# A recurrent mixer's 64x64 inverses: block transposes moved from the matmul array to VectorE, and output products regrouped

## The chip, the cores and the metric

One core of a Trainium2 chip runs the whole program; the other cores are idle. The metric is the device time of one execution in microseconds (us). The engines that matter here are TensorE (PE: the matmuls, with the loading of their stationary operands shown apart as PEld), VectorE (DVE) and ScalarE (ACT). Each works through its own list of instructions in a fixed order, and they wait for one another by semaphores. Matmul results land in PSUM, a memory of eight banks; DVE and ACT carry them from there to on-chip memory (SBUF).

## The reference

The input x has 512 tokens of 1024 features. Three blocks follow one another: a macaron block (half a SwiGLU feed-forward, a mixer, half a feed-forward), a second block with a gated recurrence and spatial gating, and a third with two more layers. All is in float32. The change lies in the first block's mixer alone, and there in its recurrent half:

```python
p = h @ w_in                                  # r, k, v and the inputs of small low-rank products
w = -softplus(-(w0 + tanh(w_lo) @ w2)) - 0.5
a = sigmoid(a0 + a_lo @ a2)
kk = normalised (k * k_k) per head;  bh = kk * a;  decay = exp(-exp(w))
def step(state, inp):                          # 8 heads, state 64 x 64, 512 tokens
    sa = einsum('bhvk,bhk->bhv', state, -kk_t)
    state = state * w_t[:, :, None, :] + sa[..., None] * b_t[:, :, None, :] + v_t[..., None] * k_t[:, :, None, :]
    return state, einsum('bhvk,bhk->bhv', state, r_t)
o = normalised per head, plus a bonus, times a gate
```

The other half of the mixer is sliding-window attention; both halves go through w_out onto the residual.

## The kernel before, in words

**The dense products.** Every large product (`dense_steps`, lines 348 to 365) splits float32 into two float32r parts and issues three matmuls with 512 moving columns for each K tile: L359, L360 and L361. They are called a triple below. The weights come by DMA into `raw`, are split by ACT (L335) and DVE (L336), and stand in `whi` and `wlo`.

**The recurrence.** Tokens are cut into 8 chunks of 64, heads into 4 pairs. Inside a chunk the recurrence needs the inverse of a unit triangular 64x64 matrix, one for each head and chunk. `head` (lines 867 to 974) computes one head's eight inverses at once: tile X (128 partitions x 4 x 64) holds the eight transposed inverses, chunk j,e on partition half e. It starts from diagonal blocks of 4 (two rounds of matmuls at L928, two updates at L929) and doubles the block size four times: blocks of 8, 16, 32, 64. A doubling, called a level below, takes W = mask * (ak' X) (matmuls L942, DVE L945), then X -= T' W on the odd blocks (matmuls L949, DVE L951; at the last level DVE L957 and ACT L958 write the result to `xb`). T is X transposed, so it has to be made anew ahead of every level. That is `turned()`, called four times for each of the eight heads, 32 times in all: for each of the eight 64x64 blocks a product with an identity, L921 in transpose mode for the blocks on partitions 0 to 63 and L919 as an ordinary float32 matmul for those on 64 to 127, alternating; then ACT copies all from PSUM to T (L922). As the doubling goes, X is block-diagonal with blocks of at most 32 whenever it is turned.

**States and outputs.** `states` (from line 977) makes, for a pair of heads, three groups of small products over the chunks (L991), a chain of six steps from chunk to chunk (matmul L1008, DVE L1009), and the outputs `po`: for each of 2 heads and 8 chunks two products into the same 64x64 patch, one from `gv` and `rb` with 128 rows and 64 columns (L1018), then one from the state `z` and `cf` with 64 rows and 64 columns (L1019), one chunk after the other. `finish` (from line 1025) normalises and gates what they give.

A float32 matmul of the program runs as two MATMUL instructions on PE, a product in transpose mode as one; so L919 counts 256 instructions in the trace, L921 128, L942 and L949 512 each, L1018 and L1019 128 each. The profile's "64*64" or "128*64" is the part of the array that an instruction uses (rows*columns).

**What sets the order.** Five generators are stepped in turn by `rounds` in the pattern D Z A D H P H A: D the dense projections (one triple a step; at the end the product with w_out), Z the states, A the attention, P what is done per token, H the heads. The order of emission is thus fixed in the program, with dense triples between the heads' small products as long as D has work. D stands still where the product with w_out has to wait for the states of the third pair. A scheduler then orders each engine's list near that emission. Each engine keeps its list's order whatever is ready.

Of the kernel before, what the change touches and what calls it, by code (L numbers as in the profile page):

```python
# [12 lines left out]
AF = mybir.ActivationFunctionType  # L13
# [13 lines left out]
# ---------------------------------------------------------------- layout and shape-only constants  # L27

def col_blocks(w, cols=None):
    """(K, N) -> (N/128, 128, K/128 * 128): one 128-column block holds its K tiles side by side."""  # L30
    k, n = w.shape
    return np.ascontiguousarray(
        w.reshape(k // P, P, n // P, P).transpose(2, 1, 0, 3).reshape(n // P, P, (k // P) * P))


def wide_blocks(w):
    """(1024, N) -> (N/512, 4, 128, 2 * 512): 512 columns of two K tiles to a block"""
    n = w.shape[1]
    return np.ascontiguousarray(
        w.reshape(4, 2, P, n // S, S).transpose(3, 0, 2, 1, 4).reshape(n // S, 4, P, 2 * S))  # L40


def masks_1():
    t = np.arange(P)
    # rows are tokens of a chunk, on either half of the partitions
    s, u = (t % 64)[:, None], np.arange(64)[None, :]
    out = {"up": s < u, "upi": s <= u, "m4u": (s // 4 == u // 4) & (s < u), "m4l": (s // 4 == u // 4) & (s > u), "id2": s == u}
    for l in range(2, 6):
        # columns of the odd blocks only
# [16 lines left out]
class Pack:  # L66
    """Column-packed (128, n) array with named column ranges."""
# [25 lines left out]
def down(w):  # L93
    """(F, 1024) -> list over groups of F tiles of (8, 128, n * 128)"""
# [33 lines left out]
def layout_3(i, a, vec, at):  # L128
# [26 lines left out]
    c = Pack()  # L155
# [5 lines left out]
    # retention: even and odd dimensions of a head in tiles of their own  # L161
# [6 lines left out]
    # the last head's rows by themselves, whole  # L168
# [21 lines left out]
def layout(inputs):  # L190
# [27 lines left out]
    # the last two recurrent heads by themselves  # L218
# [13 lines left out]
# ---------------------------------------------------------------- the program  # L232

class Model:
# [21 lines left out]
    def setup(self):  # L256
# [27 lines left out]
        # the first blocks of weights come between the tiles of x  # L284
# [8 lines left out]
    def banks(self, **n):  # L293
        """the PSUM banks of a phase: how many to a tag"""
# [10 lines left out]
    def spill(self):  # L305
        """the residual waits in DRAM; its place on chip serves the mixer meanwhile"""
# [8 lines left out]
    def sooner(self, n):  # L315
        """n instructions ahead of its place in the scheduler's order"""
# [4 lines left out]
    # -- dense products ------------------------------------------------  # L321
# [5 lines left out]
    def weights(self, src):  # L327
        """a (128, n <= 1024) block of weights as an exact sum of two float32r parts"""
# [10 lines left out]
    def dense(self, blocks, act, tag="d"):  # L339
        """blocks: list of (weights src, first K tile of act, n K tiles); returns the accumulated tile"""  # L340
# [7 lines left out]
    def dense_steps(self, blocks, act, tag="d", every=NKT):  # L348
        """the same, with a pause after every so many K tiles"""
# [26 lines left out]
    # -- norms ---------------------------------------------------------  # L376
    def ln_exp(self):
        """the one table set that serves both Ln and Exp"""
# [5 lines left out]
    def in_turn(self, i):  # L384
        """ACT issues the instructions given here in their order, to change tables seldom"""
# [5 lines left out]
    def newton(self, y, m, tmp):  # L391
        """one step for y = m ** -0.5"""
# [6 lines left out]
    def rsqrt_(self, out, m, tmp):  # L399
        """out = m ** -0.5 for positive m"""  # L400
        nc = self.nc
        with self.ln_exp():
            # Ln serves 2 ** -64 to 2 ** 64
# [4 lines left out]
    def rsqrt_few(self, out, m, tmp):  # L408
        """the same for a few numbers per partition"""
# [3 lines left out]
    def norm_in(self, g):  # L413
        """split of x * g and the running sum of squares, K tile by K tile"""
# [15 lines left out]
    def sum_sq(self, acc, x, k):  # L430
        """acc += x * x, from k = 0 on; returns the square"""
# [9 lines left out]
    def token_sums(self, acc, out, scale, bias):  # L441
        """out (128 tokens, 4 blocks) = scale * sum over the partitions of acc (128, 512), or of several, + bias"""
# [9 lines left out]
    def spread(self, pool, rt, tag):  # L452
        """(128 tokens, 4 blocks) -> (128, 512) with that row on every partition"""
# [17 lines left out]
    def rstd(self, acc, eps, meanwhile=lambda: None):  # L471
        """1 / sqrt(mean over the 1024 features + eps), on every partition; meanwhile(): products
        that keep the tensor engine busy until it can be spread"""
# [8 lines left out]
    def norm_twice(self, pool, g1, g2, eps1, eps2):  # L482
        """the split of the residual times both gains, and a function for when the first product is under
        way (meanwhile: as in rstd): it returns the factor per token that completes both norms, and a function that puts the norm
        by g1 in the residual's place"""
# [47 lines left out]
    def token_dense_steps(self, w, act, evac, step=None):  # L533
        """products with tokens on partitions: w is (N / 512, 4, 128, 2 * 512), two K tiles to a block;
        evac(column block, token block, tile). Token block n is tokens 128 n.., or n, n + 4, .. by step"""
# [18 lines left out]
    def conv(self, out, b, w, bias, j, n):  # L554
        """causal depthwise convolution of width 4 over the tokens; b has three zeros in front"""
# [6 lines left out]
    def residual(self, w, act, c0=0):  # L562
        """x += act @ w, over the K tiles of w from column c0 of its blocks"""
# [5 lines left out]
    # -- feed-forward --------------------------------------------------  # L569
# [49 lines left out]
# ---------------------------------------------------------------- RWKV-7 and sliding-window attention  # L619
# [9 lines left out]
def weave(*gens, tc=None, ahead=None):  # L629
    """emits the generators' steps in turn until all have ended; ahead: by how many  # L630
    instructions each goes before its place in the scheduler's order"""
# [12 lines left out]
def rounds(gens, order):  # L644
    """steps of the named generators in the given order, again and again until all have ended"""
# [6 lines left out]
class Mixer1:  # L652
# [22 lines left out]
    # banks for the heads, for what is per token, and for states and outputs  # L675
# [9 lines left out]
    def shifted(self, j, out, swap=False):  # L685
        """projection tile j, scaled by the norm, mixed with the token before;
# [290 lines left out]
    def states(self, i, q):  # L977
# [35 lines left out]
        for h in range(2):  # L1013
# [6 lines left out]
            if h == 0:  # L1020
                yield
# [1204 lines left out]
```

## Time and profile before

| what | value |
|---|---|
| median of the three runs | 2947.56 us (2942.62 to 2950.02) |
| span of the profiled execution, first to last instruction | 2940.8 us |
| the profiled execution's own time | not listed apart; the runs lie 1.8 to 9.2 us above the span |
| PE busy | 2897.1 us, 99% of the span |
| DVE busy | 1675.2 us, 57% |
| ACT busy | 1174.8 us, 40% |
| mean clock granted to PE | 0.979 |
| stretch of the mixer's recurrence | about 410 to 845 us from the start |

The share of busy time of PE counts a matmul from its start to its modelled end, and neighbours overlap. What an instruction costs PE's list is therefore read here from the timeline, as the distance from its start to the start of the next row; this is called its pitch. The granted clock (PEclk) is 1.00 at full speed.

### The profile page before, as it was taken

Reading aid. Unit: us, or ns where it says so; the run is one execution under the profiler, and the core shown is the slowest. Engines: PE = TensorE matmul, PEld = TensorE weight load, DVE = VectorE, ACT = ScalarE, POOL = GpSimd, SP = SyncE. Lnnn points to the kernel's source line nnn. Section 1 sums busy time; section 2 is a strip of 40 time slices with the busy share of each in tenths; the row PEclk is TensorE's granted clock in tenths of the full one; section 3 lists DMA queues with packets and bytes.
Section 4 is the critical chain, followed back from the end, with each engine's and each line's share of the span. In section 5 each row is a group of like instructions: output and inputs, shape, how many; then the busy total and the mean of one; then the engine's idle time right before and its main releaser. Section 6 shows DMA issues by size and latency. Waiting matters only on the chain. (4 is left out here: it accounts for less than half of the span.)

```text
span 2940.8 us, 37140 instructions
## 1 busy us (share of the span) xinstructions
PE 2897.1 (99%) x14918; PEld 2331.2 (79%) x14918; DVE 1675.2 (57%) x2762; ACT 1174.8 (40%) x1813; POOL 78.9 (3%) x167
## 2 busy tenths in 40 slices
PE   8999999999999999999999999999999999999998
PEld 7888867777768888877888878888887777888887
DVE  5444565556254344768535697545834895555456
ACT  4222353444232222456423334434527544343333
POOL 0000000000000000000000011110000000000000
PEclk9999999999699999999999999999989999999999
DMA  4333331001023333432233344444212543322232
GB/s 139 94 101 93 93 110 37 23 27 43 20 65 95 99 95 95 143 95 79 85 102 129 108 128 153 137 135 124 92 45 79 172 143 122 115 79 79 69 108 76
DMA packets 83870, 281.24 MB, mean 96 GB/s; under 512 B 10097, under 2 KB 10609, under 8 KB 82929
## 3 DMA queue, kind: packets, MB, share of 16 engines
q1 hardware_dynamic: 76464, 255.28, 28.1%
q0 software_dynamic: 5888, 18.09, 1.8%
q10 hardware_dynamic: 1344, 5.49, 0.5%
q8 instruction: 117, 1.92, 0.3%
q14 instruction: 57, 0.46, 0.0%
HBM read 254.44 MB, written 23.07 MB: 94 GB/s over the span
## 5 line engine op out<-in xcount | busy, mean ns | idle before, releaser
L335 ACT CAST whi<-raw 128x1024 fp32r<-128x1024 f32 (+4 forms) x454 | 450.5, 992 | 1194.9 <-PE ps_d L360 795.2
L359 PE MATMUL ps_d<-xhi,whi 128*128 128x512 f32 x1896 | 759.2, 401 | 12.9 <-ACT whi L335 8.4
L361 PE MATMUL ps_d<-xhi,wlo 128*128 128x512 f32 x1896 | 746.0, 394 | 3.4 <-DVE wlo L336 3.4
L360 PE MATMUL ps_d<-xlo,whi 128*128 128x512 f32 x1896 | 746.3, 394 | 0.0
L336 DVE TENSOR_TENSOR wlo<-raw,whi 128x1024 fp32r<-128x1024 f32 (+4 forms) x454 | 521.9, 1149 | 167.5 <-ACT whi L335 166.6
L359 PEld LDWEIGHTS ps_d<-xhi,whi 128*128 128x128 f32 x1896 | 358.3, 189 | 93.8 <-ACT whi L335 8.8
L361 PEld LDWEIGHTS ps_d<-xhi,wlo 128*128 128x128 f32 x1896 | 358.6, 189 | 80.4 <-DVE wlo L336 4.8
L360 PEld LDWEIGHTS ps_d<-xlo,whi 128*128 128x128 f32 x1896 | 358.9, 189 | 74.5 <-issue 3.7
L359 PE MATMUL ps_d<-hh,whi 128*128 128x512 f32 x608 | 237.5, 391 | 0.6 <-ACT hh L373 0.6
L361 PE MATMUL ps_d<-hh,wlo 128*128 128x512 f32 x608 | 237.2, 390 | 0.5 <-DVE wlo L336 0.5
L360 PE MATMUL ps_d<-hl,whi 128*128 128x512 f32 x608 | 237.2, 390 | 0.3 <-DVE hl L374 0.3
L361 PEld LDWEIGHTS ps_d<-hh,wlo 128*128 128x128 f32 x608 | 114.2, 188 | 25.0 <-DVE wlo L336 1.4
L359 PEld LDWEIGHTS ps_d<-hh,whi 128*128 128x128 f32 x608 | 114.2, 188 | 24.9 <-ACT hh L373 1.0
L360 PEld LDWEIGHTS ps_d<-hl,whi 128*128 128x128 f32 x608 | 114.2, 188 | 24.6 <-DVE hl L374 1.1
L594 DVE TENSOR_TENSOR hb<-ps_d,rstd 128x512 f32<-128x512 f32 x44 | 30.4, 691 | 136.2 <-PE ps_d L361 136.2
L601 DVE SCALAR_TENSOR_TENSOR x<-ps_d,x 128x512 f32<-128x512 f32 x48 | 33.2, 692 | 116.3 <-PE ps_d L361 116.3
L359 PE MATMUL ps_d<-mixhi,whi 128*128 128x512 f32 x224 | 89.0, 397 | 1.0 <-DVE x L1641 0.8
L360 PE MATMUL ps_d<-mixlo,whi 128*128 128x512 f32 x224 | 88.3, 394 | 0.0
L361 PE MATMUL ps_d<-mixhi,wlo 128*128 128x512 f32 x224 | 88.1, 393 | 0.0
L593 DVE TENSOR_TENSOR ha<-ps_d,rstd 128x512 f32<-128x512 f32 x44 | 30.4, 692 | 95.8 <-PE ps_d L361 93.2
L438 DVE TENSOR_TENSOR acc<-acc,sq 128x512 f32<-128x512 f32 x67 | 46.1, 688 | 25.7 <-ACT sq L437 25.1
L1445 DVE TENSOR_TENSOR x<-ps_d,x 128x512 f32<-128x512 f32 x32 | 22.0, 689 | 61.3 <-PE ps_d L361 61.3
(698 smaller groups left out, 4441.3 us busy)
## 6 DMA issues: line engine op xcount, KB each, us to landing
raw<-in_ffn_gu_dram SPq DMA_DIRECT2D x88, 512.0 KB, 3.6
raw<-in_w_in_dram SPq DMA_DIRECT2D x64, 512.0 KB, 3.6
raw<-in_ffn_dn_dram SPq DMA_DIRECT2D x32, 512.0 KB, 3.6
raw<-in_w_up_dram SPq DMA_DIRECT2D x32, 512.0 KB, 3.7
raw<-in_w_down_dram SPq DMA_DIRECT2D x32, 512.0 KB, 4.0
raw<-in_ret_in_dram SPq DMA_DIRECT2D x32, 512.0 KB, 3.3
raw<-in_ab_in_dram SPq DMA_DIRECT2D x28, 512.0 KB, 3.4
raw<-in_ret_v_dram SPq DMA_DIRECT2D x16, 512.0 KB, 3.3
```

Source lines behind the costliest of these rows:

```text
L335: nc.scalar.copy(hi[:, :n], raw[:, :n])
L336: nc.vector.tensor_sub(lo[:, :n], raw[:, :n], hi[:, :n].bitcast(F32))
L359: self.nc.tensor.matmul(ps, lhsT=hi[:, w], rhs=ah, start=first, stop=False)
L360: self.nc.tensor.matmul(ps, lhsT=hi[:, w], rhs=al, start=False, stop=False)
L361: self.nc.tensor.matmul(ps, lhsT=lo[:, w], rhs=ah, start=False, stop=last)
L438: nc.vector.tensor_add(acc, acc, sq)
L593: nc.vector.tensor_mul(a, pg, r)
L594: nc.vector.tensor_mul(b, pu, r)
L601: nc.vector.scalar_tensor_tensor(out=xm, in0=po, scalar=0.5, in1=xm, op0=ALU.mult, op1=ALU.add)
L1445: nc.vector.tensor_add(xm, po, xm)
```

## The change

Two edits in the recurrent half of the mixer. `turned()` no longer goes through PE, PSUM and ACT: one DVE instruction transposes the 32x32 blocks of X into T, each block in its place, for all eight matrices. Because X is block-diagonal with blocks of at most 32 there, this is the transpose that the level needs. In `states` the 16 products of `gv` and `rb` come first, then a step of the generator ends, then the 16 products of `z` and `cf`. So that the patches of one PSUM bank can stand open meanwhile, only the first product of each head carries the flag that starts an accumulation and only the last the flag that ends it. The number of steps of each generator is the same as before. The change also drops comments and docstrings, most of them without moving a line; from `turned()` on, lines stand 7 lower than before (L942 is now L935, L949 now L942, L1018 now L1011), and from `finish` on 3 lower.

```diff
         def turned():
-            pt = half(self.pm())
-            for j, e, he in each:
[...]
-                if e:
-                    mm(pt[he, j], lhsT=X[he, j], rhs=m.const("ident")[he, he], start=True, stop=True)
-                else:
-                    nc.tensor.transpose(pt[he, j], X[he, j], m.const("ident")[he, he])
-            nc.scalar.copy(T, pt)
+            nc.vector.transpose(T.rearrange("p j t -> p (j t)"), X.rearrange("p j t -> p (j t)"))
...
         po = self.pz()
         for h in range(2):
             hs = HALF[h]
             rb = q["rb%d" % h]
             for c in range(8):
+                mm(po[hs, c * 64:c * 64 + 64], lhsT=gv[:, c, hs], rhs=rb[:, c], start=(c == 0), stop=False,
+                   skip_group_check=True)
+        yield
+        for h in range(2):
+            hs = HALF[h]
+            for c in range(8):
                 cs = slice(c * 64, c * 64 + 64)
-                mm(po[hs, cs], lhsT=gv[:, c, hs], rhs=rb[:, c], start=True, stop=False)
-                mm(po[hs, cs], lhsT=z[hs, c], rhs=cf[hs, cs], start=False, stop=True)
-            if h == 0:
-                yield
+                mm(po[hs, cs], lhsT=z[hs, c], rhs=cf[hs, cs], start=False, stop=(c == 7), skip_group_check=True)
         self.step[i] = 2
         yield from self.finish(i, q, po)
```

On PE, in the first level of the first two heads, the list before ran as follows (`x8` stands for eight equal rows; X, T, W and ak are the tiles named above, `xhi` and `whi` belong to a dense triple, `cst` holds the identity):

```order
L942 MATMUL ps_m<-X,ak 64x32 x8
L949 MATMUL ps_m<-W,T 64x32 x8
L359 MATMUL ps_d<-xhi,whi 128x512
L360 MATMUL ps_d<-xlo,whi 128x512
L361 MATMUL ps_d<-xhi,wlo 128x512
...
L949 MATMUL ps_m<-W,T 64x32 x8
L921 MATMUL ps_m<-cst,X 64x64
L919 MATMUL ps_m<-cst,X 64x64
...
L359 MATMUL ps_d<-xhi,whi 128x512
```

The same place now:

```order
L935 MATMUL ps_m<-X,ak 64x32 x8
L942 MATMUL ps_m<-W,T 64x32 x8
L359 MATMUL ps_d<-xhi,whi 128x512
L360 MATMUL ps_d<-xlo,whi 128x512
L361 MATMUL ps_d<-xhi,wlo 128x512
...
L942 MATMUL ps_m<-W,T 64x32 x8
L359 MATMUL ps_d<-xhi,whi 128x512
```

The pairs of L921 and L919 (four pairs to a group) are gone and nothing has come in their place on PE; the triples stand where they stood. In the recurrence's whole stretch of PE's list the dense matmuls are 584 before and 584 now.

On DVE, at the same place, the list before (L929 are the updates of X in blocks of 4, L951 those of a level, L1056 belongs to the attention):

```order
L929 SCALAR_TENSOR_TENSOR X<-ps_m,m_2450 128x256 x2
L1056 TENSOR_TENSOR z<-ps_d,rstd 128x512
L929 SCALAR_TENSOR_TENSOR X<-ps_m,m_2450 128x256
L336 TENSOR_TENSOR wlo<-raw,whi 128x1024
L945 TENSOR_TENSOR W<-ps_m,m_2450 128x128 x2
L951 TENSOR_TENSOR X<-X,ps_m 128x32x4 x2
```

DVE's list at that place now, where L922 is the old L929, L938 the old L945 and L944 the old L951:

```order
L922 SCALAR_TENSOR_TENSOR X<-ps_m,m_2450 128x256 x2
L915 STREAM_TRANSPOSE T<-X 128x256
L1053 TENSOR_TENSOR z<-ps_d,rstd 128x512
L922 SCALAR_TENSOR_TENSOR X<-ps_m,m_2450 128x256
L336 TENSOR_TENSOR wlo<-raw,whi 128x1024
L915 STREAM_TRANSPOSE T<-X 128x256
L938 TENSOR_TENSOR W<-ps_m,m_2450 128x128 x2
L944 TENSOR_TENSOR X<-X,ps_m 128x32x4
L915 STREAM_TRANSPOSE T<-X 128x256
```

Each transpose stands right behind the update of X that it reads, or one instruction later, and ahead of the W of the same level.

On PE, the first pair's outputs before (`gv`, `rb`, `z` and `cf` as above):

```order
L361 MATMUL ps_d<-xhi,wlo 128x512
L1018 MATMUL ps_z<-rb,gv 64x64
L1019 MATMUL ps_z<-cf,z 64x64
...
L359 MATMUL ps_d<-xhi,whi 128x512
```

PE's list for the same outputs now, where L1011 is the old L1018 and L1018 the old L1019:

```order
L1011 MATMUL ps_z<-rb,gv 64x64 x16
L359 MATMUL ps_d<-xhi,whi 128x512
L360 MATMUL ps_d<-xlo,whi 128x512
L361 MATMUL ps_d<-xhi,wlo 128x512
...
L1018 MATMUL ps_z<-cf,z 64x64 x16
```

Before, a run of eight alternating pairs stood here, and the second head's run came some rows later; now 16 products of one kind stand together, and the 16 of the other kind come where the second run was.

## The prediction

> **What bounds the kernel now.** I read the page's totals, the windows over the mixer, PE's waits there, and the groups and timeline of the instructions that go.
>
> ```profile
> span 2940.8 us, 37140 instructions
> PE 2897.1 (99%) x14918; PEld 2331.2 (79%) x14918; DVE 1675.2 (57%) x2762; ACT 1174.8 (40%) x1813; POOL 78.9 (3%) x167
> ```
>
> ```profile
> 425.00:450.00 25.00, 25.00 (x317) 18.59 (x316) 9.70 (x21) 8.03 (x15) 0.15 (x1) 1.00 0.10 24
> 700.00:725.00 25.00, 24.25 (x327) 19.34 (x325) 21.78 (x68) 11.18 (x32) 0.00 (x0) 1.00 0.17 70
> 725.00:750.00 25.00, 25.00 (x193) 17.80 (x192) 6.38 (x19) 4.58 (x12) 0.00 (x0) 0.65 0.13 38
> 750.00:775.00 25.00, 25.00 (x202) 16.71 (x201) 7.56 (x16) 7.52 (x15) 0.15 (x1) 0.67 0.00 1
> 775.00:800.00 25.00, 25.00 (x194) 19.08 (x191) 6.77 (x13) 6.23 (x16) 0.00 (x0) 0.73 0.13 38
> 400.00:850.00 450.00, 444.59 (x3769) 318.41 (x3767) 234.30 (x571) 170.63 (x352) 1.69 (x15) 0.90 0.11 35
> ```
>
> Columns: stretch, its length, busy time of PE, PEld, DVE, ACT and POOL, granted clock, DMA share, GB/s. PE is occupied for 444.6 of the mixer's 450 us while DVE has 234 and ACT 171. All the same the DVE is nearly full in one place, 21.8 of 25 us from 700 on.
>
> ```profile
> PE ps_m L928 <- DVE X L929: 0.5, 1, 0.5
> ```
>
> ```profile
> DVE W L945 <- PE ps_m L942: 53.8, 26, 4.8
> ACT T L922 <- PE ps_m L919: 77.5, 31, 6.6
> ```
>
> Columns: who waited for whom, total us, times, longest. On the inverse and the outputs PE waited for another engine once, 0.5 us; DVE and ACT waited for PE. So inside the mixer time is PE's list added up, at the clock that it is granted. What leaves that list leaves the time, unless PE then has to wait.
>
> **The transposes, PE.** The groups that go, and one of them in the timeline at full clock and one at the lower:
>
> ```profile
> L919 PE MATMUL ps_m<-cst,X 64*64 64x64 f32 x256 | 43.3, 252 | 0.0
> L921 PE MATMUL ps_m<-cst,X 64*64 64x64 f32 x128 | 31.9, 250 | 0.0
> L922 ACT COPY T<-ps_m 128x256 f32<-128x256 f32 x32 | 11.9, 372 | 77.5 <-PE ps_m L919 77.5
> ```
>
> ```profile
> 431.12 0.24 PE L921 MATMUL ps_m<-cst,X 64*64 64x64 f32 x1
> 431.29 0.33 PE L919 MATMUL ps_m<-cst,X 64*64 64x64 f32 x2
> ...
> 432.58 0.33 PE L919 MATMUL ps_m<-cst,X 64*64 64x64 f32 x2
> 432.83 0.50 PE L359 MATMUL ps_d<-xhi,whi 128*128 128x512 f32 x1
> ...
> 747.84 0.31 PE L921 MATMUL ps_m<-cst,X 64*64 64x64 f32 x1
> ...
> 750.00 0.47 PE L919 MATMUL ps_m<-cst,X 64*64 64x64 f32 x2
> 750.40 1.22 PE L1035 MATMUL ps_m<-wsg,lora 128*128 128x512 f32 x1
> ```
>
> The busy time, 75.2 us, counts overlaps twice. By pitch a group lasts 432.83 - 431.12 = 1.71 us at full clock and 750.40 - 747.84 = 2.56 at the lower. Added over all 384 instructions, from 431.12 to 779.61, the pitches give 53.6 us, 1.68 to each of 32 groups. The triples around them stay, and the number of switches between dense and small runs is about the same in both lists (123 and 121 dense runs), so nothing is gained there: **-53.6 us**.
>
> **The transposes, DVE.** 32 instructions of 128x256 come; ACT's 11.9 us go. No row shows a DVE transpose. Its nearest rows are operations of that size from SBUF to SBUF, the far one the scan of twice the size:
>
> ```profile
> L1113 DVE TENSOR_SCALAR sc<-sc,asm 128x256 f32<-128x256 f32 x24 | 7.4, 350 | 0.2
> L901 DVE TENSOR_TENSOR X<-X,m 128x256 f32<-128x256 f32 x8 | 3.3, 412 | 0.0
> L749 DVE TENSOR_TENSOR_SCAN L<-m,sgp 128x512 f32<-128x512 f32 x3 | 3.7, 1218 | 0.0
> ```
>
> Bounds 0.35 and 1.22 us; I take L901's 0.41, which reads the same tile: 13.2 us on DVE, beside PE. [...]
>
> As latency the new way is shorter: before, T came after PE's 1.7 us and ACT's 0.37; now T stands on DVE right behind the X that it reads, and the products of X with ak need no T. Queued behind each transpose are W of the other head, the attention's small operations and the chain of states, each 0.4 us later. Where triples stand between, one takes 0.80 us at its end, so this is hidden:
>
> ```profile
> 797.36 0.50 PE L359 MATMUL ps_d<-amix,whi 128*128 128x512 f32 x1
> 797.70 0.39 PE L360 MATMUL ps_d<-amix,whi 128*128 128x512 f32 x1
> 797.93 0.40 PE L361 MATMUL ps_d<-amix,wlo 128*128 128x512 f32 x1
> 798.16 0.40 PE L359 MATMUL ps_d<-k,whi 128*128 128x512 f32 x1
> ```
>
> The cover is gone between about 705 and 760 us, where dense work stands still until the third pair's states are through, and the fourth pair's heads run almost alone. PE's groups there were long enough to hide DVE's answers; shorter ones are not. In the new list that place has about ten handovers from DVE or ACT: X to the two rounds in blocks of 4, z to the chain of states, X, W and T to the first levels, the attention's softmax to its products. The one wait of this kind before cost 0.5 us; ten make **+5 us** (bounds 0 and, at 1.22 us each, 12).
>
> **The outputs.** Before and the nearest rows of one kind only:
>
> ```profile
> 519.23 0.33 PE L1018 MATMUL ps_z<-rb,gv 128*64 128x64 f32 x2
> 519.49 0.33 PE L1019 MATMUL ps_z<-cf,z 64*64 64x64 f32 x2
> ...
> 523.33 0.50 PE L359 MATMUL ps_d<-xhi,whi 128*128 128x512 f32 x1
> 526.17 0.68 PE L897 MATMUL ps_m<-x 64*64 64x64 f32 x16
> 526.78 0.50 PE L359 MATMUL ps_d<-xhi,whi 128*128 128x512 f32 x1
> ...
> 795.53 1.90 PE L991 MATMUL ps_m<-gv,bkT 128*64 128x64 f32 x32
> 797.36 0.50 PE L359 MATMUL ps_d<-amix,whi 128*128 128x512 f32 x1
> ```
>
> ```profile
> L1018 PE MATMUL ps_z<-rb,gv 128*64 128x64 f32 x128 | 24.6, 283 | 0.0
> L1019 PE MATMUL ps_z<-cf,z 64*64 64x64 f32 x128 | 24.6, 281 | 0.0
> ```
>
> 32 instructions took 523.33 - 519.23 = 4.10 us, 128 ns each; over all 256, to their end near 828, the pitches add up to 39.6 us, some of it at the lower clock. Runs of one shape: L991, a chunk at a time in the same columns, 1.83 / 32 = 57 ns; L897, alternating between two corners of the array, 0.61 / 16 = 38 ns. The new runs stay in one corner for 16 instructions, which is L991's manner; 256 x 57 = 14.6 us. **-25 us.** Bounds: 38 ns for all gives 9.7 and -29.9; no gain at all, 0, is a rival.
>
> **The clock.** Inside the slow windows the clock is 0.50 (the first row below, with PE's busy time in 5 us); at 0.90 over 450 us, 90 us ran so. It hit where the removed groups stood: 0.65 to 0.73 from 725 to 800, where four output runs and eight transposes stand close; but 425 to 450 has four transpose groups and 1.00. Three dense matmuls cost 787.55 - 786.27 = 1.28 us there, and three times 0.23 = 0.69 at full clock (797.70 to 798.16 above):
>
> ```profile
> 740.00:745.00 5.00, 5.00 (x34) 0.50 0.00 0
> ...
> 786.27 0.63 PE L360 MATMUL ps_d<-a,whi 128*128 128x512 f32 x1
> ...
> 787.55 0.63 PE L360 MATMUL ps_d<-e,whi 128*128 128x512 f32 x1
> ```
>
> That is 1.85 times; small products lost less, 2.56 against 1.71, 1.5 times. Of the 90 us some 30 are the removed groups themselves, counted above. The other 60 would take about 60 / 1.65 = 36 at full clock (1.65 lies between 1.5 and 1.85), so 24 us are at stake. I take a good half back, **-13 us** (bounds -24 and +10, about as much lost anew).
>
> Sum: -53.6 + 5 - 25 - 13 = -86.6 against the span of 2940.8. The runs lie 2 to 9 us above the span, the median 6.8; less 86.6 the median becomes **2861 us**.
>
> **Rivals.**
>
> *The clock comes back whole.* The stretches at 0.50 end with the work that I think brings them on. For it: the windows from 725; against it, 425 to 450. -24 in place of -13: 2850. [...]
>
> *DVE becomes the wait.* If a transpose takes 1.22 us, or the heads' chains answer late also where triples stand, each of 32 levels lets PE wait 0.8 us: 26 us in place of 5 gives 2882. For it: DVE's 21.8 of 25 us at 700; against: 234 of 450 overall.
>
> *Grouping is worth nothing,* because what spaces L1018 and L1019 is that both write one PSUM patch or one bank, and the new runs still do: 2861 + 25 = 2886. Against it: L991 writes one bank at 57 ns.
>
> *Slower: the lower clock spreads.* PE's small gaps and the unbroken small runs could hold the clock at half through the mixer. The mixer's 584 dense matmuls at + 0.20 us are 117 us. Of its 435 us, less 584 x 0.27 for these and 79 that go, 200 are small work, at half as much again + 100. Less the 24 paid now that is + 193, and 2947.6 - 73.6 + 193 = 3067. It decides from 74 us on, which takes some 190 microseconds more at half clock. Against it: 700 to 725 holds small float32 products almost alone, at 1.00.
>
> **Chances.** Forecast 0.54, clock whole 0.20, DVE 0.13, grouping nothing 0.08, clock spreading 0.05 (0.03 past the point, 0.02 near it). About 0.3% is what a measurement can tell from no change: faster 0.95, same 0.02, slower 0.03. The range takes in 2850 and 2886 with some microseconds for the runs' spread and L897's pitch: 2839 to 2888.
>
> **What would show it.** The transposes on DVE at 0.35 to 0.5 us; the output runs of 32 instructions at about 1.9 us; PE's waits for DVE in the mixer of 3 to 10 us, nearly all where dense work stands still; the next feed-forward starting about 85 us sooner; the mean clock up from 0.979. Wrong would be PE waits above 20 us, output runs near 4 us, or windows at 0.50 in new places. The other blocks should not move.

## The result, and the profile after

The changed kernel takes 2834.82 us (median of 4 runs, 2832.53 to 2837.08), the kernel before 2945.59 (4 runs, 2942.62 to 2950.02). The ratio is 0.9627, with a 95% interval of 0.9613 to 0.964: 110.8 us less. Faster was right, but the forecast of 2861 is 26 us too high, and its range began 4 us above the result.

The profiled execution took 2831.0 us, 109.8 less than before. The page's totals, after:

```profile
span 2831.0 us, 36332 instructions
PE 2786.5 (98%) x14534; PEld 2258.0 (80%) x14534; DVE 1682.0 (59%) x2794; ACT 1164.0 (41%) x1781; POOL 79.3 (3%) x167
```

The 384 matmul rows of the transposes are gone, PE's busy time is 110.6 us less, DVE's only 6.8 us more and ACT's 10.8 less. The mean granted clock rose from 0.979 to 0.995.

The windows over the mixer after (stretch, length, busy time of PE, PEld, DVE, ACT and POOL, granted clock, DMA share, GB/s):

```profile
425.00:450.00 25.00, 25.00 (x330) 19.00 (x329) 14.39 (x39) 7.89 (x17) 0.15 (x1) 1.00 0.15 44
625.00:650.00 25.00, 23.79 (x268) 18.18 (x267) 19.56 (x54) 13.94 (x35) 0.00 (x0) 1.00 0.29 104
650.00:675.00 25.00, 24.51 (x364) 19.39 (x363) 19.92 (x65) 9.82 (x27) 0.00 (x0) 1.00 0.03 7
400.00:740.00 340.00, 334.43 (x3374) 246.61 (x3374) 237.57 (x598) 157.31 (x318) 1.85 (x15) 1.00 0.14 45
```

The clock reads 1.00 in every stretch; before it was 0.65 to 0.73 from 725 to 800 and 0.90 over the whole. DVE is now busy for 19 to 20 of 25 us around 650, and still PE stands idle no longer than before: 340.00 - 334.43 = 5.6 us against 450.00 - 444.59 = 5.4.

The groups that answer to the removed and the moved ones (line, engine, operation, tiles, shapes, count, busy time, mean ns, idle time before):

```profile
L915 DVE STREAM_TRANSPOSE T<-X 128x256 f32<-128x256 f32 x32 | 13.8, 437 | 0.2
L1011 PE MATMUL ps_z<-rb,gv 128*64 128x64 f32 x128 | 7.8, 225 | 0.0
L1018 PE MATMUL ps_z<-cf,z 64*64 64x64 f32 x128 | 7.6, 221 | 0.0
```

A transpose takes 0.437 us on DVE, where 0.41 was estimated. The outputs' busy time fell from 49.2 us (24.6 twice) to 15.4. One run of them in the timeline (start, duration, engine, line, tiles, count):

```profile
501.31 1.90 PE L1011 MATMUL ps_z<-rb,gv 128*64 128x64 f32 x32
503.14 0.50 PE L359 MATMUL ps_d<-xhi,whi 128*128 128x512 f32 x1
```

The pitch is (503.14 - 501.31) / 32 = 57 ns, as the forecast had it. PE's waits in the mixer that before did not have (total us, times, longest):

```profile
PE ps_m L984 <- ACT gv L966: 0.9, 2, 0.6
PE ps_m L921 <- DVE asm L1106: 0.5, 1, 0.5
PE ps_d L359 <- ACT amix L373: 0.5, 1, 0.5
```

They come to 1.9 us, against the 0.5 that went with the old wait at L928.

**Where the time went.** I added the pitches of all PE rows of the mixer, from its first `wsg,lora` product to its last `k,whi` product, by kind. In us:

| kind of row | before | after | difference |
|---|---|---|---|
| transposes (old L919, L921) | 53.6 | 0 | -53.6 |
| outputs (L1011, L1018) | 39.6 | 14.4 | -25.2 |
| dense triples | 185.3 | 171.0 | -14.4 |
| levels (L935, L942) | 42.9 | 37.3 | -5.6 |
| everything else, with PE's waits | 137.4 | 130.1 | -7.4 |
| the whole stretch | 458.9 | 352.7 | -106.2 |

The last three kinds are the same instructions in both kernels, in nearly the same order. They lost 27.4 us although the waits in them grew by 1.4, so 28.8 are faster work, and the clock is what changed: before had 92 us at 0.50 between 459 and 859 (3.4 of them, from 855, behind the mixer's end), and after has none until 749.1, after the mixer's end. Taken row by row, the shared rows that ran at 0.50 before, wholly or in part, take 36.0 us in place of 63.1; all other shared rows of the stretch take 302.3 in place of 302.6. Before's clock fell ten times inside the mixer, and the rows that went or were regrouped stood ahead of every fall: the last 3.4 us before it hold 1.3 to 2.3 us of transposes, or at least 3.3 of outputs, or, once, 1.4 and 1.0 of both.

Up to the mixer the two traces agree within 0.2 us. Behind it the last blocks run 3.6 us shorter, and 2.6 of that is the clock again: between 2155 and 2177 before is 1.3 us slower, in a stretch at 0.50 of 20.5 us where after has 17.1, and near 2437 it is 1.3 us slower in a short stretch that after doesn't have. The second in windows, before and then after (length, PE busy, clock, DMA share, GB/s):

```profile
2434.00:2440.00 6.00, 4.43 (x14) 0.72 0.34 134
2325.00:2331.00 6.00, 4.43 (x20) 1.00 0.44 165
```

The length of the first stretch and the presence of short ones behind it differ also between the kernels below, which are all alike behind the mixer; so I count these 2.6 us as luck and not as a gain of the change. The other 1.0 lies between 1725 and 1762, about half of it a wait for `wlo` that after doesn't have.

### The profile page after: what moved, and what is told of

It is laid out like the page before. It is cut to its first block, busy times and chain, and to the rows that moved or that the text cites. A ratio compares the mean times of both kernels' runs of the same rounds, so it can differ in the third digit from the quotient of the medians.

```text
span 2831.0 us, 36332 instructions
## 1 busy us (share of the span) xinstructions
PE 2786.5 (98%) x14534; PEld 2258.0 (80%) x14534; DVE 1682.0 (59%) x2794; ACT 1164.0 (41%) x1781; POOL 79.3 (3%) x167
## 3 DMA queue, kind: packets, MB, share of 16 engines
q8 instruction: 114, 1.87, 0.3%
## 5 line engine op out<-in xcount | busy, mean ns | idle before, releaser
L360 PEld LDWEIGHTS ps_d<-hl,whi 128*128 128x128 f32 x608 | 114.1, 188 | 24.5 <-DVE hl L374 1.1
```

Of the source, the lines that this page charges most:

```text
L360: self.nc.tensor.matmul(ps, lhsT=hi[:, w], rhs=al, start=False, stop=False)
```

## The experiments

The forecast's own theory was that the removed groups lower the clock and that about half of it returns. The rivals left after the result: all of it hangs on transpose mode, all of it hangs on the outputs' alternation, or any dense run of slow, alternating small products lowers the clock. Where an expectation gives theories by a letter, it says what each forecasts. Each run stood beside runs of the kernel before on the same chip.

### Each part alone

Transposes on DVE, outputs alternating as before:

```diff
             for c in range(8):
-                mm(po[hs, c * 64:c * 64 + 64], lhsT=gv[:, c, hs], rhs=rb[:, c], start=(c == 0), stop=False,
-                   skip_group_check=True)
-        yield
-        for h in range(2):
-            hs = HALF[h]
-            for c in range(8):
                 cs = slice(c * 64, c * 64 + 64)
-                mm(po[hs, cs], lhsT=z[hs, c], rhs=cf[hs, cs], start=False, stop=(c == 7), skip_group_check=True)
+                mm(po[hs, cs], lhsT=gv[:, c, hs], rhs=rb[:, c], start=True, stop=False)
+                mm(po[hs, cs], lhsT=z[hs, c], rhs=cf[hs, cs], start=False, stop=True)
+            if h == 0:
+                yield
```

> The changed kernel with the outputs back in alternating order (L1011 and its z products chunk by chunk), the transposes on VectorE. At full clock the 256 output instructions cost 128 ns each, 32.8 us against the 14.4 of the changed kernel: 2835 + 18 = 2853 us. Theory A (any dense run of slow, alternating small products brings the lower clock on): some of the 90 us at 0.50 stay, where the output runs stand; mean clock 0.985 to 0.992, 2858 to 2870 us. Theory B (only products in transpose mode bring it on): mean clock 0.995, 2853 us. Theory C (only the output runs bring it on): clock as before, 0.979 to 0.983, about 2878 us.

Measured: 2864.52 us (2862.35 to 2866.29), ratio 0.9732 [0.9709, 0.9755], clock 0.990.

Outputs grouped, transposes back on PE and ACT:

```diff
-            nc.vector.transpose(T.rearrange("p j t -> p (j t)"), X.rearrange("p j t -> p (j t)"))
+            pt = half(self.pm())
+            for j, e, he in each:
+                if e:
+                    mm(pt[he, j], lhsT=X[he, j], rhs=m.const("ident")[he, he], start=True, stop=True)
+                else:
+                    nc.tensor.transpose(pt[he, j], X[he, j], m.const("ident")[he, he])
+            nc.scalar.copy(T, pt)
```

> The changed kernel with turned() back on TensorE (transpose mode and ordinary matmul alternating), the outputs grouped. At full clock the 32 groups cost 51 us: 2835 + 51 = 2886 us. Theory A: a part of the low clock stays, mean clock 0.983 to 0.992, 2892 to 2908. Theory B: the low clock stays nearly whole, 0.979 to 0.983, about 2912. Theory C: 0.995 and 2886.

Measured: 2910.21 us (2895.16 to 2920.39), ratio 0.9883 [0.9844, 0.9923], clock 0.985.

The two ratios give 2.7 and 1.2 per cent, 79 and 34 us; both together give 110. The second's four runs lie 25 us apart, at mean clocks from 0.981 to 0.991, so its part is known to some 12 us. Within that the parts add up, with no large gain that only the pair makes. Theory A's ranges hold the first kernel and miss the second by 2 us; theories B and C each miss the first by 11 us or more. Each brought clock back beside its own rows: where before had 92 us at 0.50, the first has 27 (3.4 of them at 406) and the second 51. The mixer in windows, first the kernel with the transposes alone, then the one with the outputs alone (length, PE busy, clock, DMA share, GB/s):

```profile
400.00:775.00 375.00, 367.50 (x3393) 0.97 0.13 42
400.00:820.00 420.00, 412.25 (x3775) 0.94 0.12 38
```

By pitches the transposes alone take 53.6 us off (the outputs still 35.9), the outputs alone 24.5 (15.1 left). The first one's windows over an output run (length, PE busy, clock, DMA share, GB/s):

```profile
510.00:515.00 5.00, 5.00 (x45) 1.00 0.01 3
515.00:520.00 5.00, 5.00 (x59) 0.57 0.00 0
520.00:525.00 5.00, 5.00 (x33) 0.75 0.10 17
690.00:695.00 5.00, 5.00 (x31) 0.50 0.00 0
695.00:700.00 5.00, 5.00 (x29) 0.50 0.00 0
```

With no transpose of the inverse left on PE the clock still falls around alternating outputs. So neither the transposes nor the outputs are the one cause.

### Is it transpose mode?

Two kernels put the transposes back on PE in other forms, with the outputs grouped. In the first all eight are ordinary products with the identity:

```diff
-            nc.vector.transpose(T.rearrange("p j t -> p (j t)"), X.rearrange("p j t -> p (j t)"))
+            pt = half(self.pm())
+            for j, e, he in each:
+                mm(pt[he, j], lhsT=X[he, j], rhs=m.const("ident")[he, he], start=True, stop=True)
+            nc.scalar.copy(T, pt)
```

> turned() on TensorE again, but all eight products of a group ordinary float32 matmuls with the identity (16 instructions, no transpose mode), copied by ScalarE; outputs grouped. If the alternation of transpose mode and matmul made the groups slow: 16 instructions at 34 to 40 ns, 0.55 to 0.64 us a group, 18 to 20 us in all, clock 0.995, 2835 + 19 = 2854 us. If the work itself costs 1.6 us a group: 2886 us or more, and a lower clock.

Measured: 2854.91 us (2849.4 to 2854.98), ratio 0.9693 [0.9665, 0.9721], clock 0.993. In the second the kinds are those of before, four in transpose mode and four products, but one kind after the other instead of in turn:

```diff
-            nc.vector.transpose(T.rearrange("p j t -> p (j t)"), X.rearrange("p j t -> p (j t)"))
+            pt = half(self.pm())
+            for j, e, he in each:
+                if e == 0:
+                    nc.tensor.transpose(pt[he, j], X[he, j], m.const("ident")[he, he])
+            for j, e, he in each:
+                if e == 1:
+                    mm(pt[he, j], lhsT=X[he, j], rhs=m.const("ident")[he, he], start=True, stop=True)
+            nc.scalar.copy(T, pt)
```

> turned() on TensorE as before the change, but its four products in transpose mode first and its four ordinary matmuls behind them (12 instructions as before, copied by ScalarE); outputs grouped. If only the change from one mode to the other is slow (eight changes a group before, two now): about 0.6 to 0.8 us a group, 19 to 26 us in all, 2855 to 2862 us. If a product in transpose mode is slow by itself (178 ns of pitch before): 1.0 to 1.3 us a group, 2868 to 2880 us. If the order makes no difference: as with the outputs alone grouped, 2910 us.

Measured: 2865.04 us (2859.97 to 2867.36), ratio 0.9726 [0.9707, 0.9746], clock 0.993. Its timeline over one group, and its windows over all of them:

```profile
433.93 0.41 PE L918 MATMUL ps_m<-cst,X 64*64 64x64 f32 x4
434.27 0.67 PE L921 MATMUL ps_m<-cst,X 64*64 64x64 f32 x8
434.88 0.50 PE L359 MATMUL ps_d<-xhi,whi 128*128 128x512 f32 x1
```

```profile
425.00:500.00 75.00, 75.00 (x798) 1.00 0.10 34
500.00:600.00 100.00, 99.95 (x1019) 1.00 0.11 35
600.00:700.00 100.00, 99.31 (x1224) 1.00 0.12 41
700.00:775.00 75.00, 73.68 (x648) 1.00 0.17 55
```

The timeline of the kernel with ordinary products only has its first group as one row:

```profile
434.25 0.63 PE L917 MATMUL ps_m<-cst,X 64*64 64x64 f32 x16
```

Three things follow. First, the price of a group was mostly the turn from one kind to the other: 1.71 us in turn, 434.88 - 433.93 = 0.95 us in two blocks (0.84 on the average of 32), 0.60 as sixteen rows of one kind. That is why PE could have had the same transposes for 19 us in place of 54, with no DVE at all. Second, the gain of DVE over the best form tried on PE is 20 us (2854.91 to 2834.82), not 54. Third, the same 128 rows in transpose mode as before stand in the second kernel, and the clock is 1.00 from 425 to 775. Transpose mode by itself does not lower it here, in groups of four rows of 85 ns; with the same rows in turn, and the outputs grouped just so, the clock stood at 0.50 for 51 us. As the account of before's low clock, transpose mode alone does not hold.

### Does DVE's work lie hidden?

Each transpose on DVE is issued twice, the second writing the same values again:

```diff
             nc.vector.transpose(T.rearrange("p j t -> p (j t)"), X.rearrange("p j t -> p (j t)"))
+            nc.vector.transpose(T.rearrange("p j t -> p (j t)"), X.rearrange("p j t -> p (j t)"))
```

> The changed kernel with every VectorE transpose issued twice (the second writes the same T again): 32 more instructions of 0.44 us, 14 us more on VectorE. If VectorE's work is hidden beside TensorE: 2835 us, within 0.1%. If the heads' chains wait for VectorE: up to 2849 us, with new waits of TensorE for T or W.

Measured: 2842.0 us (2839.91 to 2843.39), ratio 0.9655 [0.9633, 0.9677], clock 0.994, about 7 us above the changed kernel. Its second group of transposes and the one new wait on DVE in the inverse:

```profile
L916 DVE STREAM_TRANSPOSE T<-X 128x256 f32<-128x256 f32 x32 | 13.8, 433 | 0.1
```

```profile
PE ps_m L943 <- DVE W L939: 1.5, 1, 1.5
```

The mixer takes 6.9 us more than in the changed kernel. Some 3 of them are a stretch of 7 us at 0.50 at 406, where the inverse begins. The doubled transposes are not shown to cause it, because the kernel with the kinds in two blocks has it too, with no transpose on DVE (first this kernel, then that one; length, PE busy, clock, DMA share, GB/s):

```profile
405.00:413.00 8.00, 6.10 (x13) 0.57 0.38 106
405.00:413.00 8.00, 6.74 (x15) 0.57 0.39 131
```

That leaves about 4 us, 1.5 of them the wait, for the 13.8 us added to DVE. So the single transposes lie hidden for the most part beside PE; of as much work again, less than a third shows.

### What spaces the outputs?

Grouping could have helped because the tile shape no longer changes, or because two products in succession no longer write the same patch of PSUM. This kernel has the transposes on DVE and keeps the alternation, but each `z` product comes one chunk late (the edit as against the kernel with the transposes alone; the step between the heads stays):

```diff
-            for c in range(8):
-                cs = slice(c * 64, c * 64 + 64)
-                mm(po[hs, cs], lhsT=gv[:, c, hs], rhs=rb[:, c], start=True, stop=False)
-                mm(po[hs, cs], lhsT=z[hs, c], rhs=cf[hs, cs], start=False, stop=True)
+            for c in range(9):
+                if c < 8:
+                    mm(po[hs, c * 64:c * 64 + 64], lhsT=gv[:, c, hs], rhs=rb[:, c], start=(c == 0), stop=False,
+                       skip_group_check=True)
+                if c:
+                    cs = slice(c * 64 - 64, c * 64)
+                    mm(po[hs, cs], lhsT=z[hs, c - 1], rhs=cf[hs, cs], start=False, stop=(c == 8),
+                       skip_group_check=True)
```

> The transposes on DVE, and the two kinds of output products alternating as before, but each z-cf product comes one chunk late, so that two products in succession never write the same patch of PSUM. If it is the change of tile shape (128*64 to 64*64) that spaces the products, they stay at 128 ns a row and the kernel is where the transposes alone were: 2858 to 2870 us, granted clock about 0.990. If it is the accumulation onto the patch written just before, the rows come at 57 to 60 ns as in the grouped runs, and the kernel is near 2835 (2830 to 2842), clock about 0.995.

Measured: 2870.62 us (2868.5 to 2872.85), ratio 0.9756 [0.9739, 0.9772], clock 0.988. Its timeline (each product shows as two rows):

```profile
503.26 0.33 PE L1012 MATMUL ps_z<-rb,gv 128*64 128x64 f32 x2
503.52 0.32 PE L1016 MATMUL ps_z<-cf,z 64*64 64x64 f32 x2
503.77 0.33 PE L1012 MATMUL ps_z<-rb,gv 128*64 128x64 f32 x2
504.03 0.33 PE L1016 MATMUL ps_z<-cf,z 64*64 64x64 f32 x2
```

503.77 - 503.26 = 0.51 us for four rows, 128 ns each, as before. Same patch or not makes no difference here. What is left is the change of shape between 128*64 and 64*64, which both alternating kernels have after every second row and the grouped one doesn't. (The 6 us above the kernel that alternates without the delay go with its clock: 44 us at 0.50 against 27.) If that is all of the difference, the price here is 2 x (128 - 57) = 142 ns for each change, an estimate from the two pitches; no run changes the shape alone.

### What lowers the clock?

Read to 0.1 us, the stretches at 0.50 inside the mixers are whole multiples of 3.41 us: 3.4, 6.8, 10.2, 13.7 and 23.9 us in before. So are the stretches at 1.00 between them (61.4, 20.5, 92.2 us), so that within one run the changes of the clock lie on a fixed grid. A step of that grid, 23.9 / 7 = 3.41 us, is called a window below. What a window holds ahead of a fall was open. From the timelines I added the moving columns of every matmul row (64 for an output row, 512 for a dense one) over the window ahead of each fall. In before the ten falls inside the mixer have 496 to 807 per us; the poorest window of the changed kernel from 425 to 720 has 844, and no fall. So my theory at this point (D): a window with fewer than about 800 moving columns per us brings the clock of 0.50, whatever the instructions are. The kernel with narrow columns, below, was made to test it; the one that comes first was made ahead of the theory, to see whether the length of an unbroken slow run matters, and is read by it here.

Outputs in turn again, but split into runs of two chunks with steps of the generators between:

```diff
...
+                mm(po[hs, cs], lhsT=gv[:, c, hs], rhs=rb[:, c], start=True, stop=False)
+                mm(po[hs, cs], lhsT=z[hs, c], rhs=cf[hs, cs], start=False, stop=True)
+                if c % 2 and (h == 0 or c < 7):
+                    yield
```

> The changed kernel with the outputs in alternating order again, but in runs of two chunks with a step of the generators (a dense triple and the heads' small products) between them, where the kernel with the transposes alone had runs of eight chunks. The 256 instructions cost the same 128 ns each at full clock, so 2853 us. If the length of an unbroken slow run brings the lower clock on: mean clock 0.994 or more and 2850 to 2856 us, against 0.990 and 2864.5 us with long runs. If the slow instructions count wherever they stand: 0.990, 2862 to 2868 us. The states end later, so the stretch without dense work may move; waits of TensorE there would show it.

Measured: 2873.29 us (2870.74 to 2874.64), ratio 0.9756 [0.9742, 0.9771], clock 0.987: 9 us above the kernel that keeps the alternating outputs in one piece, and above both ranges expected. Its windows:

```profile
565.00:570.00 5.00, 5.00 (x26) 0.50 0.00 0
690.00:695.00 5.00, 5.00 (x27) 0.50 0.27 92
695.00:700.00 5.00, 5.00 (x52) 0.50 0.00 0
```

Spreading didn't help: it moved the dense triples, so that a stretch without outputs became poor too. Ahead of the fall at 562 the levels wait for DVE (timeline; in brackets PE's idle time and what ended it):

```profile
557.89 0.66 PE L942 MATMUL ps_m<-W,T 64*64 64x32 f32 x16 [0.93 <-DVE W L938]
559.42 0.54 PE L935 MATMUL ps_m<-X,ak 64*64 64x32 f32 x12 [0.88 <-DVE X L944]
```

Next, grouped outputs whose `rb`-`gv` products are cut into four of 16 columns: the same result, four times the rows, and far fewer columns per us with no change of shape and no transposes.

```diff
-                mm(po[hs, c * 64:c * 64 + 64], lhsT=gv[:, c, hs], rhs=rb[:, c], start=(c == 0), stop=False,
-                   skip_group_check=True)
+                for k in range(4):
+                    mm(po[hs, c * 64 + 16 * k:c * 64 + 16 * k + 16], lhsT=gv[:, c, hs], rhs=rb[:, c, 16 * k:16 * k + 16],
+                       start=(c == k == 0), stop=False, skip_group_check=True)
```

> The changed kernel with each grouped product of gv and rb (L1011) cut into four of 16 moving columns: 512 instructions of one shape and one mode in place of 128. At L1011's 57 ns an instruction they take 29 us, 22 more: 2857 us at full clock. Theory D (new, from the windows before each fall of the clock: TensorE is at 0.50 for 3.5 us or a multiple after a window of 3.5 us in which the moving columns of its instructions were under some 800 per us, whatever their kind; 16 columns in 57 ns are 280 per us): low windows at each of the four runs, 14 to 30 us at 0.50 in all, mean clock 0.988 to 0.992, 2862 to 2872 us. Theory A (alternation of shape or mode brings it on) and theory B (transpose mode does): no low window there, 0.994 to 0.995, 2857 us.

Measured: 2893.29 us (2891.7 to 2894.36), ratio 0.9827 [0.9812, 0.9841], clock 0.981. Its windows, first of the output tile's rows alone, then of all PE rows:

```profile
504.00:506.00 2.00, 1.77 (x31) 1.00 0.00 0
508.00:514.00 6.00, 6.00 (x63) 0.50 0.01 3
```

```profile
500.00:505.00 5.00, 5.00 (x40) 1.00 0.00 0
505.00:510.00 5.00, 5.00 (x64) 0.64 0.01 3
525.00:530.00 5.00, 5.00 (x56) 0.50 0.01 3
535.00:540.00 5.00, 5.00 (x75) 1.00 0.38 107
```

A row of 16 columns takes 1.77 / 31 = 57 ns at full clock, as one of 64 does: at these two widths the columns don't set the pitch. At 0.50 it takes 6.00 / 63 = 95 ns. The clock fell at each of the four runs of narrow products, as theory D said and A and B did not, with PE never idle at the first; but the price was beyond every expectation: 78.5 us at 0.50. The added rows cost 512 x 0.057 - 7.3 = 21.9 us at full clock; the kernel lost 58.5, so some 36.6 are the clock. A fall at 506 lasted 27 us, 18 of them after the narrow rows had ended. Why it lasted isn't shown: the windows that kept it down then had 664, 837, 671 and 1169 columns per us.

How far D holds: counted on each trace's grid, from 425 to the mixer's end in all 13 traces, the 27 falls come after windows with 290 to 807 columns per us. Of the 1201 windows after which the clock stayed at 1.00, only 15 have fewer than 800. So it matters how a poor stretch lies to the grid: in the kernel with narrow columns the window from 622.4 to 625.8 has 740 and no fall followed, the next has 291, and the clock fell at 629.2. The border isn't sharp, since one window with 620 brought no fall. It becomes sharper when a row's columns are weighted with its share of the array's 128 rows: 22 of the 27 falls then come after windows below 563, and no window below that stayed without one. Both counts were fitted to the traces that they describe; no kernel tested the second. They do not order the way back to 1.00: windows with up to 1161 columns kept the clock at 0.50, and it rose after some with fewer than 600. What exactly is counted stays open.

### Versions that could beat both

If rows in one corner of the array take 57 ns and rows alternating between corners 38 (L897, in the forecast), the heads can be interleaved. In the groups of L984 and the outputs:

```diff
-            for h in range(2):
-                hs = HALF[h]
-                gk, rb = q["gk%d" % h], q["rb%d" % h]
-                for c in range(8):
+            for c in range(8):
+                for h in range(2):
+                    hs = HALF[h]
+                    gk, rb = q["gk%d" % h], q["rb%d" % h]
...
-        for h in range(2):
-            hs = HALF[h]
-            for c in range(8):
-                cs = slice(c * 64, c * 64 + 64)
+        for c in range(8):
+            cs = slice(c * 64, c * 64 + 64)
+            for h in range(2):
+                hs = HALF[h]
```

> The changed kernel with the two heads of a pair taken in turn, chunk by chunk, in the three groups of products at L984 and in the outputs (L1011, L1018): consecutive products then write different halves of the array's columns. If a run in one place of the array is what holds these at 55 to 60 ns, and turns of place bring them to the 34 to 40 ns of L897, L907 and L921: 640 instructions by some 20 ns, 12 us less, 2823 us. If the instructions' own issue holds them: 2835 us.

Measured: 2830.75 us (2825.46 to 2831.11), ratio 0.9609 [0.9593, 0.9624], clock 0.992. By pitches L984 fell from 22.9 to 14.9 us and the outputs from 14.4 to 8.8, together -13.6; the time fell by 4. Its windows show where the rest is:

```profile
650.00:655.00 5.00, 5.00 (x33) 1.00 0.02 3
655.00:660.00 5.00, 4.74 (x24) 0.54 0.00 0
660.00:665.00 5.00, 5.00 (x55) 0.50 0.00 0
665.00:670.00 5.00, 4.64 (x121) 0.93 0.01 3
```

There are 10 us at 0.50 that the changed kernel doesn't have: the window ahead holds 744 columns per us. Another 7 us at 0.50 stand at 406, as in the kernels shown above. Together these rows take 7.5 us more than in the changed kernel. They need not come in every run: one of the four took 2825.46 us, at a clock of 0.994. The same for the outputs alone, L984 as in the changed kernel:

```diff
-        for h in range(2):
-            hs = HALF[h]
-            rb = q["rb%d" % h]
-            for c in range(8):
-                mm(po[hs, c * 64:c * 64 + 64], lhsT=gv[:, c, hs], rhs=rb[:, c], start=(c == 0), stop=False,
+        for c in range(8):
+            for h in range(2):
+                hs = HALF[h]
+                mm(po[hs, c * 64:c * 64 + 64], lhsT=gv[:, c, hs], rhs=q["rb%d" % h][:, c], start=(c == 0), stop=False,
...
```

> The kernel with the heads interleaved, but only in the outputs; the groups at L984 stand as in the changed kernel. The outputs take 8.8 us in place of 14.4, so 2829 us if the clock stays at 0.995. If the interleaving itself, and not the chance of where the windows fall, cost the other kernel its clock in the stretch without dense work: 0.992 and 2832 to 2835 us.

Measured: 2830.28 us (2828.2 to 2831.18), ratio 0.9612 [0.9596, 0.9628], clock 0.994. Its timeline:

```profile
501.36 1.15 PE L1010 MATMUL ps_z<-rb,gv 128*64 128x64 f32 x32
502.45 0.50 PE L359 MATMUL ps_d<-xhi,whi 128*128 128x512 f32 x1
```

(502.45 - 501.36) / 32 = 34 ns in place of 57, the outputs 8.7 us in place of 14.4, and nothing given back in the mixer, where the clock reads 1.00 throughout: 4.5 us less than the changed kernel, where 5.7 were to be had. And both interleavings with the dense work dealt out differently, the second dense step one place later in the round of generators:

```diff
-                   'DZADHPHA')
+                   'DZAHDPHA')
```

> The kernel with the heads interleaved everywhere (2831 us, 11 us of it at 0.50 in the stretch without dense work, 7.5 at the mixer's start), and the second dense triple of each round moved between the two steps of the heads, so that single triples stand between small groups in place of two together. Theory D: fewer windows under 800 columns, 0.994 or more in the mixer, 5 us less. Against it: some 30 more changes between dense and small work at 0.2 us, 6 us more. 2822 to 2834 us.

Measured: 2831.73 us (2831.55 to 2833.76), ratio 0.962 [0.9605, 0.9634], clock 0.993. The stretch at 655 is gone, but the 7 us at 0.50 at the mixer's start stay, and PE has a wait of 2.3 us, where the kernel with both interleavings had 1.1 and the changed kernel none:

```profile
PE ps_m L957 <- DVE xb L950: 2.3, 1, 2.3
```

So three versions lie at 2830 to 2832. The one with interleaved outputs is the simplest of them; its 4.5 us are 0.16%, and its interval overlaps the changed kernel's, so that it beats it is likely and not shown.

## Why the prediction was right and wrong

**Right: what bounds, and what leaves it.** PE's list added up, and what left it left the time: the transposes' 53.6 us whole, the outputs 25.2 for 25. The transposes took 0.437 us on DVE (0.35 to 0.5 forecast), the output runs 1.83 us for 32 rows (about 1.9), the next feed-forward began 106.3 us sooner (about 85).

**Wrong: the clock, -13.** This is the step that failed, and in both of its factors. "A good half" was to come back, since 425 to 450 has the same groups at 1.00; all of it came back, the 88.7 us at 0.50 inside the mixer to none. And the 24 us at stake were too few: 26.6 of the 88.7 us were the removed groups' own, and the other 62 shrank by 28.8 to 33, a factor of 1.87, that of the dense triples (1.85) and not the 1.65 I had put in the middle. The term measured -28.8, outside its bound of -24. The row that I held against a full return was read the wrong way: four groups at 1.00 showed that one group among dense work is not enough, not that the groups were innocent. By the counts above it took a window of 3.41 us that was poor as a whole, 496 to 807 columns per us; transposes and outputs stood ahead of all ten falls, and once both were gone or quicker the poorest window from 425 to 720 had 844, and none of the loss stayed.

**Wrong, smaller: waits of +5.** Ten handovers were to cost 0.5 us each. Three new waits cost 1.9 us and the old one of 0.5 went, +1.4. Around 650, where the forecast looked for them, DVE is busy for four fifths and PE still loses 0.5 to 1.2 us in 25. The kernel with every transpose doubled shows how near it was: about 4 us.

**The remainder.** 2861.0 less 15.8 (clock), 3.6 (waits) and 0.2 (outputs) is 2841.4. The blocks behind the mixer gave 3.6, which the forecast said wouldn't move: 2.6 of it are stretches at 0.50 there, luck as far as the traces show. The forecast set the median 6.8 us above the span, where the new one lies 3.8 above its own: another 3.0, which is luck too. That is 2834.8.

**The rivals.** The clock coming back whole was the right mechanism, at 2850 still 15 us too high by the same factor, waits and remainder. Transpose mode by itself wasn't the reason: the kernel with the kinds in two blocks keeps 1.00 with the same transposes. DVE as the wait fell (1.4 us, not 26), grouping for nothing fell (57 ns), and the reason behind that rival, the common PSUM patch, fell with the delayed `z` products at 128 ns. The clock spreading fell for this change; the narrow columns show that the mechanism exists, with 36.6 us. The range was built from 0.20 for the whole return with its price undersized, and reached only 11 us below 2850.

## What to carry to other kernels

Price a PE row by its pitch at full clock and count turns: a change of tile shape or of kind between small products cost more here than the products (128 ns a row in turn against 57 in one shape; 1.71 us a group of transposes in turn against 0.60 in one kind), so group by kind first, interleave array corners within a kind (34 ns a row in place of 57), and only then move work to another engine. When slow rows leave a stretch whose clock stood at one half, take the clock's whole loss there as coming back, the same work at full clock (here 88.7 us at 0.50 went to none), and put the half return into the range. Look for windows of about 3.4 us in which PE streams little (the falls here came after 290 to 807 columns per us), even while it reads as fully busy; a rearrangement that makes one can eat its own gain, as with both interleavings, where 13.6 us of pitch became 4 of time. And don't read a difference of some 3 us between two such kernels as an effect before comparing their stretches at 0.50 far from the edit: they differed here by that much with no cause in the edit.

## What the runs showed of the hardware that I had not expected

- PE was 100% busy and still fell to a clock of 0.50 (in before, from 725 to 750: 25.00 of 25.00 us busy, at 0.65 in the mean). In these mixers the clock fell after windows of 3.41 us with 290 to 807 moving columns per us (full dense work has 512 in 0.23 us, some 2200), for whole multiples of 3.41 us on a grid that was fixed within a run, and once it stayed down for 18 us after the narrow rows ahead of the fall had ended.
- A row of 16 columns cost the same 57 ns as one of 64 in the same corner of the array (narrow columns 1.77 / 31, the changed kernel 1.83 / 32); one of 64 cost 34 ns where two corners took turns (outputs interleaved, 1.09 / 32).
- A transpose-mode row and an ordinary product in turn, both 64*64, cost 1.71 us a group of twelve rows in before; the same rows in two blocks cost 0.84, and sixteen ordinary rows 0.60.
- Rows alternating in twos between 128*64 and 64*64 cost 128 ns each, rows of one shape 57 (142 ns a change, by estimate), and it made no difference whether both products wrote the same patch of PSUM: 128 ns either way.
